# Layout of split fp32 operands in the feed-forward blocks of a decoder trunk: high and low parts mixed by elements or by fours

## The chip, the cores and the metric

One core of a Trainium2 chip runs the whole program. The metric is the device time of one launch in microseconds; the median of several runs is given, and beside it the time of the one execution that the profiler recorded.

## The reference

The program computes two layers of a decoder trunk for 256 tokens of width 1024 in fp32. Each layer is: a half-step feed-forward block, a token mixer with memory cross-attention, a second half-step feed-forward block.

```python
def swiglu(x, w_in, w_out):
    gate, up = jnp.split(x @ w_in, 2, axis=-1)
    return (jax.nn.silu(gate) * up) @ w_out
...
for i in range(DEPTH):                                   # DEPTH = 2
    x = x + 0.5 * swiglu(rms_norm(x, ffn1_norm_g[i]), ffn1_w_in[i], ffn1_w_out[i])
    ...                                                  # mixer: mLSTM (layer 0), sliding window (layer 1)
    x = x + 0.5 * swiglu(rms_norm(x, ffn2_norm_g[i]), ffn2_w_in[i], ffn2_w_out[i])
```

`w_in` is 1024 x 5632 and `w_out` 2816 x 1024, so there are four feed-forward blocks of the same shape. They are called blocks 1 to 4 here; the first mixer (A) lies between blocks 1 and 2, the second (B) between blocks 3 and 4.

## The kernel before, in words

**Split products.** An fp32 product is computed as three matmuls of the type fp32r. Each operand is split into a high part (a copy rounded to fp32r) and a low part (the operand less its high part). `mm3` (lines 224 to 228) issues high x high (line 225), stationary high x moving low (226) and stationary low x moving high (227) into one PSUM bank. Each of the three matmuls loads its own 128 x 128 stationary operand and streams 256 moving columns; the profile lists the loads as PEld.

**Weights.** `wtile` (215) takes a raw tile `wr` of 128 x 4 x 256 values (512 KB) by DMA on SP's queue into a ring of 5 and calls `split` (206): ScalarE copies it to `wh` (211), VectorE subtracts to `wl` (212). `wh` and `wl` are separate tiles in two rings of 8. `wcols` (221) picks the tile of an input projection.

**Activations.** They are kept transposed, features on partitions, tokens along the free axis. A `Norm` object holds the normalised input of the next stage: `put` receives one of four pieces of 2 x 256 values, calls `split_gain` (239: ScalarE scales and rounds, line 132 through `act`; VectorE makes the low part, 241) into the tiles `xh` and `xl`, in two rings of 4, and sums squares (`square`, `fold`). `chain` later computes the reciprocal norm with four small matmuls, an operation on GpSimd and four broadcast matmuls (line 231). The norm's factor is applied after the products.

**A feed-forward block.** `ffn_in` (471) makes the first half: 11 groups of 256 hidden columns, for each gate and up, two weight tiles each, in all 44 weight tiles and 1056 matmuls with a weight tile as the stationary operand and `x.xh`, `x.xl` moving. After each group `hidden` (473) multiplies with the norm's factor (476), applies SiLU, multiplies gate and up (479) and splits the result (`split_plain`, 244, lines 245 and 246) into tiles `u` of 2 x 256 values. `ffn` (509) then makes the second half: for each of four output pieces six weight tiles (`KG`), 528 matmuls in all, moving the split hidden tiles. Lines 544 and 546 add the result to the residual; `nxt.put` hands it to the next norm.

**Order.** TensorE and SP run in the order in which the program is traced; a small planner (`Weave`) puts chains such as a norm's into the stream of matmuls at estimated times. The order on ScalarE and VectorE follows the tiles' dependencies, which the framework turns into semaphore waits: a tile of a ring is written again once all readers of its old contents are done.

**Where things lie.** Within a tile the values that one matmul reads are side by side: 256 moving values of 4 bytes, or 128 stationary ones. The mixers use the same helpers (`Group`, line 310 onwards; `out_proj`), in part with the activations as the stationary operand.

Of the kernel before, what the change touches and what calls it, by code (L numbers as in the profile page):

```python
# [11 lines left out]
F32R = mybir.dt.float32r  # L12
# [7 lines left out]
P = 128  # L20
T = 256
D = 1024
FF = 2816
# [32 lines left out]


WARM = 18


class Weave:
# [37 lines left out]
def tile_trunk(ctx: ExitStack, tc: tile.TileContext, a, out):  # L99
# [99 lines left out]
    def g(i):  # L199
        return gcol[:, i:i + 1]  # L200
# [2 lines left out]
    pieces = [1]  # L203
    last = [None]

    def split(src, shape):
        hi = mk(whp, shape, F32R, "wh")
        lo = mk(wlp, shape, F32R, "wl")
        n = shape[1] // pieces[0]
        for i in range(pieces[0]):  # L210
            last[0] = nc.scalar.copy(hi[:, i * n:(i + 1) * n], src[:, i * n:(i + 1) * n])  # L211
            tt(out=lo[:, i * n:(i + 1) * n], in0=src[:, i * n:(i + 1) * n],  # L212
               in1=hi[:, i * n:(i + 1) * n].bitcast(F32), op=ALU.subtract)
        return hi, lo

    def wtile(src, nk, ncol=256):
        raw = mk(wrp, [P, nk, ncol], F32, "wr")
        nc.sync.dma_start(raw, src)
        return split(raw, [P, nk, ncol])

    def wcols(w, c0, kh):
        return wtile(w.rearrange("(k p) f -> p k f", p=P)[:, kh * 4:(kh + 1) * 4, c0:c0 + 256], 4)

    def mm3(ps, wh, wl, xh, xl, start, stop):
        nc.tensor.matmul(ps, wh, xh, start=start, stop=False, skip_group_check=True)  # L225
# [13 lines left out]
    def split_gain(src, gc, hi, lo):  # L239
        act(hi, src, AF.Copy, scale=gc)  # L240
        nc.vector.scalar_tensor_tensor(out=lo, in0=src, scalar=gc, in1=hi.bitcast(F32),
                                       op0=ALU.mult, op1=ALU.subtract)

    def split_plain(src, hi, lo):
        nc.scalar.copy(hi, src)
        tt(out=lo, in0=src, in1=hi.bitcast(F32), op=ALU.subtract)
# [6 lines left out]
    def bcast_rows(ps, cols):  # L253
        for h in range(2):
            mmf(ps[:, h * P:(h + 1) * P], cols[:, h:h + 1].to_broadcast([P, P]), ident, P)

    def pair(x):
        return x.unsqueeze(1).to_broadcast([P, 2, T])


    class Norm:


        def __init__(self, gi, rows=True, half=True):
            self.gi, self.rows, self.half, self.rc = gi, rows, half, None
            self.done = False
            self.xT, self.xh, self.xl = [], [], []

        def put(self, xn):
            c2 = len(self.xT)  # L270
            hi, lo = mk(xhp, [P, 2, T], F32R, "xh"), mk(xlp, [P, 2, T], F32R, "xl")
            for m in range(2):
                split_gain(xn[:, m], g(self.gi + 2 * c2 + m), hi[:, m], lo[:, m])
            self.xh.append(hi)
            self.xl.append(lo)
            self.xT.append(xn)
            self.square(xn, c2 == 0)
            if c2 == 3:
                self.fold()
# [118 lines left out]
    x0 = Norm(G_F1)  # L398
# [69 lines left out]

    KG = [(0, 4), (4, 4), (8, 4), (12, 4), (16, 4), (20, 2)]

    def ffn_in(x, w_in, hh, hl, mid=None):

        def hidden(ps):
            t = tmp()
            for m in range(2):
                tt(out=t[:, m], in0=ps[m][:, :T], in1=x.rb, op=ALU.mult)  # L476
            act(t, t, AF.Silu)
            for m in range(2):
                tt(out=t[:, m], in0=t[:, m], in1=ps[m][:, T:], op=ALU.mult)  # L479
            hi, lo = unit(F32R), unit(F32R)  # L480
            split_plain(t, hi, lo)
            hh.append(hi)
            hl.append(lo)

        waiting = []
        for gi in range(11):
            ps = [mo(), mo()]
            for kh in range(2):
                for part in range(2):
                    wh, wl = wcols(w_in, part * FF + gi * 256, kh)  # L490
                    for m in range(2):
                        for k in range(4):
                            kc = kh * 4 + k
                            mm3(ps[m][:, part * T:(part + 1) * T],
                                wh[:, k, m * P:(m + 1) * P], wl[:, k, m * P:(m + 1) * P],
                                x.xh[kc // 2][:, kc % 2], x.xl[kc // 2][:, kc % 2],
                                start=kc == 0 and part == 0, stop=kc == 7)
# [11 lines left out]
    def ffn(x, w_in, w_out, nxt=None, mid=None):  # L509

        pieces[0] = 1
        hh, hl = [], []
        yield from ffn_in(x, w_in, hh, hl, mid)
        w = w_out.rearrange("(k p) f -> p k f", p=P)

        def products(ps, m, kg, wt, start):
            ms = slice(m * P, (m + 1) * P)
            for k in range(kg[1]):
                kc = kg[0] + k
                mm3(ps, wt[0][:, k, ms], wt[1][:, k, ms], hh[kc // 2][:, kc % 2], hl[kc // 2][:, kc % 2],  # L520
                    start=kc == 0 and start, stop=kc == 21)

        for c2 in range(4):
# [23 lines left out]
            if nxt is None:  # L547
                nc.scalar.dma_start(out[:, 2 * c2:2 * c2 + 2], xn)
            else:
                nxt.put(xn)  # L550
        wv.spawn(nxt.chain(), LAT['norm'])


# [95 lines left out]
    def mixer_a(x, nxt):  # L649
# [30 lines left out]
        gh, gl = mk(whp, [P, 8, P], F32R, "wh"), mk(wlp, [P, 8, P], F32R, "wl")  # L680
# [306 lines left out]
    with tc.manual_schedule(engines={mybir.EngineType.PE, mybir.EngineType.SP}):  # L987
        wv.run(program())
# [38 lines left out]
```

## Time and profile before

| | us |
|---|---|
| median of 3 runs | 1013.55 |
| lowest and highest | 1012.36, 1013.79 |
| the profiled execution | 1012.23 |
| its span in the trace | 1010.4 |

| engine | busy us | share of the span |
|---|---|---|
| TensorE matmuls (PE) | 998.5 | 99% |
| TensorE weight loads (PEld) | 980.2 | 97% |
| VectorE (DVE) | 655.5 | 65% |
| ScalarE (ACT) | 519.5 | 51% |
| GpSimd (POOL) | 35.7 | 4% |

Matmuls are pipelined: one that lasts 276 ns in the records does not keep the next from starting about 113 ns after it. So a busy share near 100% says that matmuls follow each other without a pause, not how dense they are; the distance between two starts says that. A row of the timeline has start, duration, engine, line, operation, output <- inputs (moving, stationary), shapes and count. A row of groups has count, busy time, mean duration in ns, and the idle time of the engine ahead of the group with what ended it.

### The profile page before, as it was taken

Reading aid. Unit: us, or ns where it says so; the run is one execution under the profiler, and the core shown is the slowest. Engines: PE = TensorE matmul, PEld = TensorE weight load, DVE = VectorE, ACT = ScalarE, POOL = GpSimd, SP = SyncE. Lnnn points to the kernel's source line nnn. Section 1 sums busy time; section 2 is a strip of 40 time slices with the busy share of each in tenths; the row PEclk is TensorE's granted clock in tenths of the full one; section 3 lists DMA queues with packets and bytes.
Section 4 is the critical chain, followed back from the end, with each engine's and each line's share of the span. In section 5 each row is a group of like instructions: output and inputs, shape, how many; then the busy total and the mean of one; then the engine's idle time right before and its main releaser. Section 6 shows DMA issues by size and latency. Waiting matters only on the chain.

```text
span 1010.4 us, 20624 instructions
## 1 busy us (share of the span) xinstructions
PE 998.5 (99%) x8594; PEld 980.2 (97%) x8594; DVE 655.5 (65%) x1063; ACT 519.5 (51%) x764; POOL 35.7 (4%) x32
## 2 busy tenths in 40 slices
PE   8999999999999999999999999999999999999998
PEld 7999999999999999999999999999987899999998
DVE  6866665577856676665558666656787766666551
ACT  7754445446656554444445544544557754454440
POOL 1200000000001000000000000000121000000000
PEclk9999999999999999999999999999999999999999
DMA  9776656666644566665676666567541347666550
GB/s 308 242 245 200 192 180 185 199 183 179 184 139 133 167 210 195 200 189 170 192 206 205 189 191 201 173 197 198 182 131 66 100 131 220 198 189 185 188 170 21
DMA packets 173204, 182.70 MB, mean 181 GB/s; under 512 B 7124, under 2 KB 168328, under 8 KB 173112
## 3 DMA queue, kind: packets, MB, share of 16 engines
q1 hardware_dynamic: 171872, 179.60, 58.3%
q10 hardware_dynamic: 1016, 1.58, 0.5%
q8 instruction: 67, 1.10, 0.5%
q0 software_dynamic: 224, 0.22, 0.2%
q14 instruction: 25, 0.20, 0.1%
HBM read 180.32 MB, written 1.05 MB: 180 GB/s over the span
## 4 chain that ended last, share of the span: by engine, by line
PE 94%; DVE 3%; ACT 1%; DMA 1%; POOL 0%; issue 0%; SPq 0%; ACTq 0%
PE bank L225 30%; PE bank L226 30%; PE bank L227 30%; PE bank L231 2%; PE bank L236 1%; ACT u L132 1%; DVE wl L212 1%; DMA wr<-in_mem_w_kv_dram 1%; PE bank L961 1%; POOL col L379 0%; DVE col L930 0%; DVE u L383 0%; DVE col L591 0%; PE bank L925 0%; DVE u L946 0%
## 5 line engine op out<-in xcount | busy, mean ns | idle before, releaser
L212 DVE TENSOR_TENSOR wl<-wr,wh 128x1024 fp32r<-128x1024 f32 (+1 forms) x347 | 414.7, 1196 | 279.8 <-ACT wh L211 279.0
L211 ACT CAST wh<-wr 128x1024 fp32r<-128x1024 f32 (+1 forms) x347 | 356.8, 1031 | 393.1 <-PE bank L226 368.9
L225 PE MATMUL bank<-xh,wh 128*128 128x256 f32 x1544 | 429.1, 278 | 0.0
L226 PE MATMUL bank<-xl,wh 128*128 128x256 f32 x1544 | 426.8, 276 | 0.0
L227 PE MATMUL bank<-xh,wl 128*128 128x256 f32 x1544 | 426.8, 276 | 0.0
L226 PEld LDWEIGHTS bank<-xl,wh 128*128 128x128 f32 x1544 | 290.3, 188 | 0.1
L225 PEld LDWEIGHTS bank<-xh,wh 128*128 128x128 f32 x1544 | 290.0, 188 | 0.1
L227 PEld LDWEIGHTS bank<-xh,wl 128*128 128x128 f32 x1544 | 289.9, 188 | 0.0
L225 PE MATMUL bank<-u,wh 128*128 128x256 f32 x896 | 249.3, 278 | 0.0
L226 PE MATMUL bank<-u,wh 128*128 128x256 f32 x896 | 247.6, 276 | 0.0
L227 PE MATMUL bank<-u,wl 128*128 128x256 f32 x896 | 247.6, 276 | 0.0
L225 PEld LDWEIGHTS bank<-u,wh 128*128 128x128 f32 x896 | 168.2, 188 | 1.9 <-issue 1.7
L226 PEld LDWEIGHTS bank<-u,wh 128*128 128x128 f32 x896 | 168.4, 188 | 0.1
L227 PEld LDWEIGHTS bank<-u,wl 128*128 128x128 f32 x896 | 168.3, 188 | 0.0
L225 PE MATMUL bank<-wh,xh 128*128 128x256 f32 x208 | 59.7, 287 | 0.0
L226 PE MATMUL bank<-wl,xh 128*128 128x256 f32 x208 | 57.9, 278 | 0.0
L227 PE MATMUL bank<-wh,xl 128*128 128x256 f32 x208 | 57.9, 278 | 0.0
L476 DVE TENSOR_TENSOR t<-bank,rb 128x256 f32<-128x256 f32 x88 | 36.6, 420 | 7.3 <-PE bank L227 7.3
L225 PEld LDWEIGHTS bank<-wh,xh 128*128 128x128 f32 x208 | 39.1, 188 | 0.5 <-issue 0.3
L226 PEld LDWEIGHTS bank<-wl,xh 128*128 128x128 f32 x208 | 39.1, 188 | 0.1
L227 PEld LDWEIGHTS bank<-wh,xl 128*128 128x128 f32 x208 | 39.0, 187 | 0.0
L479 DVE TENSOR_TENSOR t<-t,bank 128x256 f32<-128x256 f32 x88 | 32.7, 412 | 1.8 <-ACT t L132 1.8
(171 smaller groups left out, 657.5 us busy)
## 6 DMA issues: line engine op xcount, KB each, us to landing
wr<-in_ffn_w_in_dram SPq DMA_DIRECT2D x176, 512.0 KB, 3.6
wr<-in_ffn_w_out_dram SPq DMA_DIRECT2D x80, 512.0 KB, 3.5
wr<-in_a_w_in_dram SPq DMA_DIRECT2D x28, 512.0 KB, 3.9
wr<-in_b_w_in_dram SPq DMA_DIRECT2D x14, 512.0 KB, 4.6
wr<-in_a_w_out_dram SPq DMA_DIRECT2D x12, 512.0 KB, 3.3
wr<-in_b_w_out_dram SPq DMA_DIRECT2D x12, 512.0 KB, 3.4
wr<-in_ffn_w_out_dram SPq DMA_DIRECT2D x16, 256.0 KB, 2.8
wr<-in_mem_w_kv_dram SPq DMA_DIRECT2D x7, 512.0 KB, 8.0
```

The costliest lines, as they stand in the source:

```text
L132: ins = nc.scalar.activation(*args, **kw)
L211: last[0] = nc.scalar.copy(hi[:, i * n:(i + 1) * n], src[:, i * n:(i + 1) * n])
L212: tt(out=lo[:, i * n:(i + 1) * n], in0=src[:, i * n:(i + 1) * n], in1=hi[:, i * n:(i + 1) * n].bitcast(F32), op=ALU.subtract)
L225: nc.tensor.matmul(ps, wh, xh, start=start, stop=False, skip_group_check=True)
L226: nc.tensor.matmul(ps, wh, xl, start=False, stop=False, skip_group_check=True)
L227: nc.tensor.matmul(ps, wl, xh, start=False, stop=stop, skip_group_check=True)
L231: nc.tensor.matmul(ps, lhsT, rhs, start=start, stop=stop, skip_group_check=True)
L236: nc.tensor.transpose(ps, src, ident[:k, :k])
L476: tt(out=t[:, m], in0=ps[m][:, :T], in1=x.rb, op=ALU.mult)
L479: tt(out=t[:, m], in0=t[:, m], in1=ps[m][:, T:], op=ALU.mult)
L961: nc.tensor.matmul(o[es[e], cs], vr[:, i, js], pTs[e][:, src], start=i == 0, stop=i == 1, skip_group_check=True)
```

## The change

The parts of one operand are stored in another way, and each of the four blocks gets a way of its own. `SIDE` keeps high and low parts side by side, `ONES` mixes them element by element (high, low, high, low), `FOURS` in runs of four elements. A matmul then reads every second element, or every second run of four.

| block | weights, first half | weights, second half | norm's activations (offset in elements) | hidden activations |
|---|---|---|---|---|
| 1 | ONES | ONES | SIDE (64) | SIDE |
| 2 | ONES | SIDE | SIDE (0) | FOURS |
| 3 | ONES | ONES | SIDE (32) | ONES |
| 4 | SIDE | SIDE | ONES (64) | ONES |

High and low weights share one tile of 2048 elements in one ring of 8. The eight parts (four pieces, high and low) of a norm's activations share one tile of 16 x 256 + 80 elements with one buffer, written from an offset `at`. In mixed blocks `hidden` splits its two halves by one pair of operations each. Some pools are allocated in another order. The mixers keep SIDE. The number, order and shapes of matmuls and DMAs are the same.

```diff
+XPAD = 80
+SIDE, ONES, FOURS = 0, 1, 4
...
-    xhp = pool("xhp", 4)
-    xlp = pool("xlp", 4)
+    vp = pool("vp", 2)
     up = pool("up", 31)
-    vp = pool("vp", 2)
+    sp = pool("sp", 2)
+    xsp = pool("xsp", 1)
     wrp = pool("wrp", 5)
-    whp = pool("whp", 8)
-    wlp = pool("wlp", 8)
+    wp = pool("wp", 8)
     tp = pool("tp", 7)
-    sp = pool("sp", 2)
...
+    lay = [SIDE]
+    def parts(shape):
+        t, n = mk(wp, [P, 2048], F32R, "w"), shape[1] * shape[2]
+        if lay[0] == SIDE:
+            return [t[:, o:o + n].rearrange("p (k f) -> p k f", k=shape[1]) for o in (0, 1024)]
+        v = t[:, :2 * n].rearrange("p (k f e) -> p e k f", k=shape[1], e=2)
+        return [v[:, 0], v[:, 1]]
     def split(src, shape):
-        hi = mk(whp, shape, F32R, "wh")
-        lo = mk(wlp, shape, F32R, "wl")
+        hi, lo = parts(shape)
...
+    def block(wt, k, m):
+        return [w[:, k, m * P:(m + 1) * P] for w in wt]
...
+    def grouped(x, c):
+        return x.rearrange("p (g c) -> p g c", c=c) if c == FOURS else x
+    def mixes(flat, c):
+        if c == ONES:
+            v = flat.rearrange("p (m t e) -> p e m t", m=2, e=2)
+        else:
+            v = flat.rearrange("p (m g e c) -> p e m g c", m=2, e=2, c=c)
+        return v[:, 0], v[:, 1]
...
         def put(self, xn):
             c2 = len(self.xT)
-            hi, lo = mk(xhp, [P, 2, T], F32R, "xh"), mk(xlp, [P, 2, T], F32R, "xl")
+            if c2 == 0:
+                self.tile = mk(xsp, [P, 16 * T + XPAD], F32R, "xs")
+            if self.mixed:
+                c0 = self.at + 4 * c2 * T
+                hi, lo = mixes(self.tile[:, c0:c0 + 4 * T], self.mixed)
+            else:
+                hi, lo = (self.tile[:, c0:c0 + 2 * T].rearrange("p (m t) -> p m t", m=2)
+                          for c0 in (self.at + 2 * c2 * T, self.at + (8 + 2 * c2) * T))
             for m in range(2):
-                split_gain(xn[:, m], g(self.gi + 2 * c2 + m), hi[:, m], lo[:, m])
+                split_gain(grouped(xn[:, m], self.mixed), g(self.gi + 2 * c2 + m), hi[:, m], lo[:, m])
...
             hi, lo = unit(F32R), unit(F32R)
-            split_plain(t, hi, lo)
-            hh.append(hi)
-            hl.append(lo)
+            if mixed:
+                h, l = [], []
+                for m, u in enumerate((hi, lo)):
+                    u = u.rearrange("p a b -> p (a b)")
+                    u = (u.rearrange("p (t e) -> p e t", e=2) if mixed == ONES else
+                         u.rearrange("p (g e c) -> p e g c", e=2, c=mixed))
+                    split_plain(grouped(t[:, m], mixed), u[:, 0], u[:, 1])
+                    h.append(u[:, 0])
+                    l.append(u[:, 1])
+                hh.append(h)
+                hl.append(l)
+            else:
+                split_plain(t, hi, lo)
+                hh.append([hi[:, 0], hi[:, 1]])
+                hl.append([lo[:, 0], lo[:, 1]])
...
-        x1, x2, x3 = Norm(G_MIX, half=False), Norm(G_F2), Norm(G_F1 + 8)
-        x4, x5 = Norm(G_MIX + 8, rows=False), Norm(G_F2 + 8)
-        yield from ffn(x0, a["ffn1_w_in"][0], a["ffn1_w_out"][0], x1, late_constants)
+        x1, x2, x3 = Norm(G_MIX, half=False), Norm(G_F2, at=0), Norm(G_F1 + 8, at=32)
+        x4, x5 = Norm(G_MIX + 8, rows=False), Norm(G_F2 + 8, mixed=ONES)
+        yield from ffn(x0, a["ffn1_w_in"][0], a["ffn1_w_out"][0], x1, late_constants, (ONES, ONES))
         yield from mixer_a(x1, x2)
-        yield from ffn(x2, a["ffn2_w_in"][0], a["ffn2_w_out"][0], x3)
-        yield from ffn(x3, a["ffn1_w_in"][1], a["ffn1_w_out"][1], x4, rope_tables)
+        yield from ffn(x2, a["ffn2_w_in"][0], a["ffn2_w_out"][0], x3, None, (ONES, SIDE), FOURS)
+        yield from ffn(x3, a["ffn1_w_in"][1], a["ffn1_w_out"][1], x4, rope_tables, (ONES, ONES), ONES)
         yield from mixer_b(x4, x5)
-        yield from ffn(x5, a["ffn2_w_in"][1], a["ffn2_w_out"][1])
+        yield from ffn(x5, a["ffn2_w_in"][1], a["ffn2_w_out"][1], None, None, (SIDE, SIDE), ONES)
```

More of the change, by code (lines that the diff above doesn't have):

```diff
@@ L261, in tile_trunk, with __init__ @@
     class Norm:
-        def __init__(self, gi, rows=True, half=True):
-            self.gi, self.rows, self.half, self.rc = gi, rows, half, None
+        def __init__(self, gi, rows=True, half=True, at=64, mixed=SIDE):
+            self.gi, self.rows, self.half, self.rc, self.at, self.mixed = gi, rows, half, None, at, mixed
             self.done = False
@@ L469, in tile_trunk, with ffn_in @@
     KG = [(0, 4), (4, 4), (8, 4), (12, 4), (16, 4), (20, 2)]
-    def ffn_in(x, w_in, hh, hl, mid=None):
+    def ffn_in(x, w_in, hh, hl, mid, mixed):
         def hidden(ps):
@@ L489, in ffn_in @@
                 for part in range(2):
-                    wh, wl = wcols(w_in, part * FF + gi * 256, kh)
+                    wt = wcols(w_in, part * FF + gi * 256, kh)
                     for m in range(2):
@@ L493, in ffn_in @@
                             kc = kh * 4 + k
-                            mm3(ps[m][:, part * T:(part + 1) * T],
-                                wh[:, k, m * P:(m + 1) * P], wl[:, k, m * P:(m + 1) * P],
+                            mm3(ps[m][:, part * T:(part + 1) * T], *block(wt, k, m),
                                 x.xh[kc // 2][:, kc % 2], x.xl[kc // 2][:, kc % 2],
@@ L507, in ffn_in, with ffn @@
                 wv.spawn(mid())
-    def ffn(x, w_in, w_out, nxt=None, mid=None):
+    def ffn(x, w_in, w_out, nxt=None, mid=None, lays=(SIDE, SIDE), mixed=SIDE):
         pieces[0] = 1
         hh, hl = [], []
-        yield from ffn_in(x, w_in, hh, hl, mid)
+        lay[0] = lays[0]
+        yield from ffn_in(x, w_in, hh, hl, mid, mixed)
+        lay[0] = lays[1]
         w = w_out.rearrange("(k p) f -> p k f", p=P)
         def products(ps, m, kg, wt, start):
-            ms = slice(m * P, (m + 1) * P)
             for k in range(kg[1]):
                 kc = kg[0] + k
-                mm3(ps, wt[0][:, k, ms], wt[1][:, k, ms], hh[kc // 2][:, kc % 2], hl[kc // 2][:, kc % 2],
+                mm3(ps, *block(wt, k, m), hh[kc // 2][kc % 2], hl[kc // 2][kc % 2],
                     start=kc == 0 and start, stop=kc == 21)
@@ L679, in mixer_a @@
         nc.sync.dma_start(raw, w.rearrange("(k p) f -> p k f", p=P)[:, :, 3072:3080])
-        gh, gl = mk(whp, [P, 8, P], F32R, "wh"), mk(wlp, [P, 8, P], F32R, "wl")
+        gh, gl = parts([P, 8, P])
         nc.vector.memset(gh.bitcast(F32), 0.0)
```

1 line of the change is left out of this document (added).

## The prediction

> **What bounds the kernel now.** I read the page first: the share of the engines, then the forty slices, then the chain that ended last.
>
> ```profile
> span 1010.4 us, 20624 instructions
> PE 998.5 (99%) x8594; PEld 980.2 (97%) x8594; DVE 655.5 (65%) x1063; ACT 519.5 (51%) x764; POOL 35.7 (4%) x32
> ...
> PEclk9999999999999999999999999999999999999999
> ...
> PE 94%; DVE 3%; ACT 1%; DMA 1%; POOL 0%; issue 0%; SPq 0%; ACTq 0%
> PE bank L225 30%; PE bank L226 30%; PE bank L227 30%; PE bank L231 2%; PE bank L236 1%; ACT u L132 1%; DVE wl L212 1%; DMA wr<-in_mem_w_kv_dram 1%; PE bank L961 1%; POOL col L379 0%; DVE col L930 0%; DVE u L383 0%; DVE col L591 0%; PE bank L925 0%; DVE u L946 0%
> ```
>
> TensorE is the bound, at full granted clock, and nine tenths of the chain are the three matmuls of `mm3` (lines 225 to 227). So I asked next whether TensorE waits for anything, and what its list of waits shows is small:
>
> ```profile
> engine line waited for: us in total, times, longest us
> PE bank L231 <- ACT u L132: 1.5, 1, 1.5
> PE bank L925 <- ACT u L132: 1.4, 1, 1.4
> PE bank L406 <- DVE t L403: 1.3, 1, 1.3
> PE bank L231 <- ACT t L603: 1.1, 1, 1.1
> PE bank L226 <- DVE wl L212: 0.9, 1, 0.9
> ```
>
> Nothing in it belongs to a feed-forward block. The time of these blocks is therefore a number of matmuls times the distance from one start to the next. A busy share hides that distance, so I read it from the timeline of TensorE, in the first feed-forward block, and shortly after a norm's small matmuls at 226 us:
>
> ```profile
> 100.05 0.28 PE L225 MATMUL bank<-xh,wh 128*128 128x256 f32 x1
> ...
> 102.09 0.28 PE L225 MATMUL bank<-xh,wh 128*128 128x256 f32 x1
> ```
>
> ```profile
> 226.02 0.28 PE L225 MATMUL bank<-xh,wh 128*128 128x256 f32 x1
> ...
> 228.02 0.28 PE L227 MATMUL bank<-xh,wl 128*128 128x256 f32 x1
> ```
>
> Between the first two rows lie 18 starts: 2.04 / 18 = 113.3 ns each. Between the second two lie 17: 2.00 / 17 = 117.6 ns. Shapes, types and clock are the same. A stretch stays at one of the two distances until other matmuls interrupt it, and the blocks run almost wholly at 113.3. Other matmuls of 4-byte data come closer:
>
> ```profile
> 270.11 0.60 PE L236 MATMUL bank<-con,u 128*128 128x128 f32 x4
> 270.54 1.03 PE L231 MATMUL bank<-kT,u 128*128 128x256 f32 x4
> ...
> L236 PE MATMUL bank<-con,u 128*128 128x128 f32 x116 | 16.7, 275 | 0.0
> L231 PE MATMUL bank<-kT,u 128*128 128x256 f32 x32 | 8.3, 382 | 1.5 <-ACT u L132 1.5
> ```
>
> Four transposes take 0.60 us from the first start to the last end; less the last one's own 0.275 and over three distances that is 108.3 ns, for 128 moving columns and a weight load of 128 x 128 for every one. The four plain fp32 products of 256 columns give (1.03 - 0.382) / 3 = 216 ns, so plain fp32 takes a column in about twice the time of the fp32r form in `mm3`. A load of 128 x 128 thus fits into 108.3 ns beside a moving stream at half the rate; beside one at full rate the pair takes 113.3 or 117.6. These extra 5.0 or 9.3 ns are what a layout could touch. My reading is that the reads of the two operands get in each other's way, the more often the more one overtakes the other; two stable values for one instruction fit a meeting of two streams that depends on how they are lined up, and fit a fixed cost of changing the weights less well.
>
> **The change part by part.** How many matmuls: one feed-forward block has 11 x 2 x 2 x 2 x 4 x 3 = 1056 in its first half and 22 x 8 x 3 = 528 in its second, 1584 in all and 6336 in four blocks. All keep their number and order. What changes is the step at which each operand is read. Side by side, the 256 moving columns cover 1024 bytes of a partition while the 128 stationary columns of the next load cover 512: one stream overtakes the other. With the weights mixed by elements the load covers 1024 bytes too, and both streams advance at one pace; their starting distance is then kept. That is so in the first halves of blocks 1, 2 and 3 (3 x 1056) and the second half of block 1 (528), where the activations stay side by side: 3696 matmuls. There I cost the full 5.0 ns: 3696 x 5.0 = 18.5 us gained. In the other 2640 (the first half of block 4 and the second halves of blocks 2, 3 and 4, with activations by fours or by elements) the paces differ again, and no row tells which way it goes: between 5.0 ns less each (13.2 us gained) and the other distance that the trace shows, 4.3 ns more each (11.4 us lost). I take no change there, since 113.3 is what nearly all such matmuls show now and is near the middle of the two ends. The new offsets of the activation tile (64, 0 and 32 elements in the first halves of blocks 1, 2 and 3, and 80 elements behind the tile) set the distance that is kept, by some hundred bytes. If one of them keeps the two streams on top of each other, that half gains nothing or goes to the other distance: 1056 matmuls are 5.3 us gained or 4.5 us lost. I take the gain for all three, as two streams in step that have given way once stay apart.
>
> The Trainium skill ("TensorE: Matmul & The Clock Gate", section "Step-by-step: what each phase is for") says that the streamed operand and the weight load have independent read ports, so that loading does not take bandwidth from a running matmul. By it the sum here would be zero, and it is a rival below; the spread of 113.3 and 117.6 for one instruction is not what I would expect from it, though no row settles that.
>
> What the other engines do for the weights and activations:
>
> ```profile
> L212 DVE TENSOR_TENSOR wl<-wr,wh 128x1024 fp32r<-128x1024 f32 x329 | 402.3, 1224 | 265.2 <-ACT wh L211 264.4
> ...
> L246 DVE TENSOR_TENSOR u<-t,u 128x512 fp32r<-128x512 f32 x44 | 30.0, 683 | 0.0
> ...
> L246 DVE TENSOR_TENSOR u<-bank,u 128x256 fp32r<-128x256 f32 x16 | 6.7, 417 | 2.8 <-ACT u L245 2.8
> ```
>
> ```profile
> L211 ACT CAST wh<-wr 128x1024 fp32r<-128x1024 f32 x329 | 345.8, 1053 | 368.5 <-PE bank L226 344.3 <-issue 7.7 <-DMA wr<-in_ffn_w_in_dram 6.5
> ...
> L245 ACT CAST u<-t 128x512 fp32r<-128x512 f32 x44 | 27.0, 613 | 0.2 <-DVE t L479 0.2
> ...
> L245 ACT CAST u<-bank 128x256 fp32r<-128x256 f32 x16 | 6.1, 382 | 7.0 <-PE bank L961 3.9 <-PE bank L231 3.0
> ```
>
> ```profile
> 100.00:150.00 50.00, 50.00 (x443) 50.00 (x443) 32.88 (x45) 24.18 (x28) 0.00 (x0) 1.00 0.62 191
> 150.00:200.00 50.00, 50.00 (x443) 50.00 (x442) 28.23 (x35) 23.84 (x29) 0.00 (x0) 1.00 0.65 188
> ```
>
> (Columns of the last: stretch, then busy time of PE, its loads, VectorE, ScalarE, GpSimd, granted clock, DMA share, GB/s. 443 matmuls touch a stretch of 50 us: 441 at 113.3 ns and two at the edges, in the first half of block 1 as in its second.) A weight tile serves 24 matmuls, 24 x 113.3 ns = 2.72 us. ScalarE needs 1.05 and VectorE 1.22 us for its two parts. Mixed by elements, ScalarE writes and VectorE reads and writes at a step of two elements. No row shows such a step: it costs nothing, or up to twice the time where each element needs a fetch that two shared before; a gain is excluded, because the number of elements is the same. I take nothing: the nearest row is line 212 itself, 1.2 ns an element, and it shows no sign that two elements are handled at once. ScalarE could even bear the double: 24.18 + 18.4 tiles x 1.05 = 43.5 us busy in 50. VectorE could not, and is a rival.
>
> `hidden` splits its tile in two parts in blocks 2, 3 and 4, 33 groups: ScalarE 2 x 382 in place of 613 ns, VectorE 2 x 417 in place of 683, 0.15 us each per 10.9 us group, beside the stream of matmuls. It costs nothing while VectorE has its 17 us free in 50; without that cover, 33 x 0.15 = 5 us.
>
> High and low weights now share one tile and one ring of 8 instead of two rings of 8. Both are still freed by the matmuls of the same tile, the low part by its last. If the interleaved parts count as overlapping, line 225 waits for VectorE's low part instead of ScalarE's high part, 1.2 us later; ScalarE's idle time in front of line 211 (344.3 of 368.5 us put down to TensorE freeing tiles) shows that the splits run up to the ring's end ahead, some seven tiles or 19 us, so nothing waits. The DMAs of the weights and SP's order stay as they are.
>
> All eight activation parts now share one tile with a single buffer. The first write of the next norm, on ScalarE's queue, waits for the last reader of the old one; behind it the splits of weights would queue, and TensorE would wait for those. But the last reader is the end of a block's first half (in a mixer, the last projection ahead of `out_proj`), and the next norm's first write comes after at least 132 matmuls of the second, 15 us later. It costs nothing. DMAs move no more bytes.
>
> **The sum** against the profiled execution: its 1012.23 us (1.83 more than its span) less 18.5 is 993.7. The median of the runs shown is 1013.55, 1.32 above it, so the forecast is 995.0 us.
>
> **The rivals.**
>
> *Full gain.* Any mix breaks the meeting of the streams and all 6336 come to 108.3: 31.7 us, 981.9 us beside the median. For it: two stable distances show that lining up matters. Against: five pairings of layouts and three offsets would all have to come out well. I count it with the forecast as the far end of one mechanism.
>
> *No change.* The 5.0 ns is a cost of each change of weights at full rate, whatever the addresses. Then nothing moves: 1013.5 us. For it: 113.3 holds for hundreds of matmuls over many tiles. Against: 117.6.
>
> *More meetings (slower).* Parts mixed by elements spread over twice the bytes, so each operand needs twice the fetches, and two streams that fetch more meet more. The price is the other distance in the trace: 6336 x 4.3 = 27.2 us, 1040.8 us. It decides as soon as more of the 6336 go up than down.
>
> *VectorE becomes the bound (slower).* At double time it needs 32.88 + 18.4 x 1.22 = 55.4 us for 50 us of matmuls in the first halves of blocks 1, 2 and 3 (119.7 us each): 3 x 12.9 = 39 us; in the second halves of 1 and 3, 28.23 + 22.5 = 50.7, another 2 us: 1055 us. It starts at 1.76 times today's 1.22 us; below that nothing shows.
>
> *A moving stream at step two runs at half rate (slower).* The nearest row is the plain fp32 product with 216 ns. Activations by elements meet it in the second half of block 3 and all of block 4, 528 + 1584 = 2112 matmuls: 2112 x 102.7 = 217 us, 1230 us. Two elements of four in every 16 bytes are still used, which speaks against it. The Trainium skill ("SBUF — State Buffer", "Specifications (TRN2)") says lines of 16 bytes need at least two hits each for full bandwidth; by elements has exactly two and by fours has four, so by it neither half rate nor anything else would be lost. No row here shows it.
>
> **How the numbers follow.** Forecast with its far end: 0.60, own range 982 to 1010. No change: 0.10. More meetings: 0.18. VectorE: 0.06. Half rate: 0.06. So faster by over 0.2% is 0.60, within it 0.10, slower 0.30; 0.2%, some 2 us, is about what a measurement of this kernel can tell from no change. The range goes from the full gain, 982, to more meetings everywhere, 1041, and leaves out the last two cases, 0.12.
>
> **What would show it.** All of block 1 and the first halves of blocks 2 and 3 should have starts near 108 ns apart. With *no change* all halves stay at 113.3; with *more meetings* those with mixed operands show 117 or more; with VectorE as the bound, TensorE waits for `wl` in its list of waits and line 212 takes over 2.1 us; with half rate, block 4 alone has starts some 216 ns apart. The forecast is wrong if the weights' layout alone, in block 1, does not shorten the distance.

## The result, and the profile after

| | before | changed |
|---|---|---|
| median, us | 1013.63 (4 runs) | 1285.58 (4 runs) |
| lowest and highest, us | 1012.36, 1013.79 | 1283.40, 1285.95 |
| span of the profiled execution, us | 1010.4 | 1283.4 |

The changed kernel is slower: ratio 1.2682, 95% interval 1.2660 to 1.2704. From the page of its profile, the span, the engines, the granted clock by slices and the chain that ended last:

```profile
span 1283.4 us, 20654 instructions
...
PE 1271.2 (99%) x8594; PEld 1211.8 (94%) x8594; DVE 663.3 (52%) x1096; ACT 539.1 (42%) x797; POOL 32.8 (3%) x32
...
PEclk9999999999999999999999999999999999999999
...
PE 92%; DVE 4%; ACT 1%; POOL 1%; DMA 1%; issue 0%; SPq 0%; ACTq 0%; POOLq 0%
```

As many matmuls as before, TensorE busy to 99%, and 272.7 of the 273.0 us by which the span is longer are TensorE's busy time. It hardly waits for another engine: its list of waits is as short as before, no entry is over 1.4 us, and the four longest, shown here, belong to other lines than the three matmuls of `mm3` (now 237 to 239).

```profile
PE bank L969 <- ACT u L131: 1.4, 1, 1.4
PE bank L243 <- ACT u L131: 1.3, 1, 1.3
PE bank L437 <- DVE t L434: 1.3, 1, 1.3
PE bank L243 <- ACT t L647: 1.1, 1, 1.1
```

So the matmuls lie further apart. The table by stretches shows where; the columns are the stretch, then busy time and (count) of PE, its loads, VectorE, ScalarE, GpSimd, then granted clock, DMA share, GB/s. The stretches lie in the first half of block 1, the second half of block 2, the first and the second half of block 3, and the first half of block 4:

```profile
100.00:150.00 50.00, 50.00 (x419) 50.00 (x418) 30.12 (x40) 23.66 (x26) 0.00 (x0) 1.00 0.57 177
500.00:550.00 50.00, 50.00 (x427) 50.00 (x426) 28.60 (x33) 23.99 (x29) 0.00 (x0) 1.00 0.62 190
600.00:650.00 50.00, 50.00 (x419) 50.00 (x418) 31.34 (x46) 24.91 (x32) 0.00 (x0) 1.00 0.58 183
700.00:750.00 50.00, 50.00 (x221) 47.18 (x219) 15.97 (x19) 12.90 (x16) 0.00 (x0) 1.00 0.32 97
1000.00:1050.00 50.00, 50.00 (x219) 45.30 (x218) 16.75 (x24) 12.51 (x16) 0.00 (x0) 1.00 0.30 95
```

The busy column says 50.00 in every row; the count tells the rows apart. It includes about two matmuls that began before the stretch, so 444 or 443 in 50 us stands for 113.3 ns between starts, 427 for 117.8, 419 for 50 / 416.6 = 120.0, and 219 for 50 / 217.1 = 230. The granted clock is 1.00 throughout. The timeline of the last stretch agrees: ten starts in 2.30 us.

```profile
1000.18 0.42 PE L238 MATMUL bank<-xs,w 128*128 128x256 f32 x1
...
1002.48 0.42 PE L239 MATMUL bank<-xs,w 128*128 128x256 f32 x1
```

By halves of the blocks, with the distances of the two traces, the extra time comes out as follows:

| where | weights, stream | matmuls | ns before | ns after | us more |
|---|---|---|---|---|---|
| first halves of 1, 2, 3; second of 1 | ONES, SIDE | 3696 | 113.3 | 120.0 | 24.6 |
| second half of 2 | SIDE, FOURS | 528 | 113.3 | 117.8 | 2.3 |
| second half of 3 | ONES, ONES | 528 | 113.3 | 228.9 | 61.0 |
| all of 4 | SIDE, ONES | 1584 | 113.3 | 230.0 | 184.8 |

The sum is 272.7 us, and the spans differ by 273.0. The table says where the time went, not yet which operand's layout costs it; and the 2.3 us of the second row may not be the layout's at all, as the section on the offsets shows.

### The profile page after: what moved, and what is told of

It is laid out like the page before. It is cut to its first block, busy times and chain, and to the rows that moved or that the text cites. A ratio compares the mean times of both kernels' runs of the same rounds, so it can differ in the third digit from the quotient of the medians.

```text
span 1283.4 us, 20654 instructions
## 1 busy us (share of the span) xinstructions
PE 1271.2 (99%) x8594; PEld 1211.8 (94%) x8594; DVE 663.3 (52%) x1096; ACT 539.1 (42%) x797; POOL 32.8 (3%) x32
## 4 chain that ended last, share of the span: by engine, by line
PE 92%; DVE 4%; ACT 1%; POOL 1%; DMA 1%; issue 0%; SPq 0%; ACTq 0%; POOLq 0%
PE bank L237 30%; PE bank L239 30%; PE bank L238 30%; PE bank L243 2%; DVE w L220 1%; POOL col L410 1%; ACT u L131 1%; DMA wr<-in_mem_w_kv_dram 1%; PE bank L248 1%; DVE col L405 0%; DVE u L990 0%; DVE col L974 0%; DVE u L414 0%; PE bank L1005 0%; DVE col L408 0%
## 5 line engine op out<-in xcount | busy, mean ns | idle before, releaser
L220 DVE TENSOR_TENSOR w<-wr,w 128x1024 fp32r<-128x1024 f32 (+1 forms) x347 | 415.0, 1197 | 488.6 <-ACT w L219 488.4
L219 ACT CAST w<-wr 128x1024 fp32r<-128x1024 f32 (+1 forms) x347 | 371.8, 1073 | 596.2 <-PE bank L239 572.0
L237 PE MATMUL bank<-xs,w 128*128 128x256 f32 x1544 | 488.6, 316 | 0.0
L239 PE MATMUL bank<-xs,w 128*128 128x256 f32 x1544 | 486.1, 315 | 0.0
L238 PE MATMUL bank<-xs,w 128*128 128x256 f32 x1544 | 484.7, 314 | 0.0
L238 PEld LDWEIGHTS bank<-xs,w 128*128 128x128 f32 x1544 | 305.8, 198 | 7.7
L239 PEld LDWEIGHTS bank<-xs,w 128*128 128x128 f32 x1544 | 305.2, 198 | 7.6
L237 PEld LDWEIGHTS bank<-xs,w 128*128 128x128 f32 x1544 | 304.6, 197 | 7.7
L237 PE MATMUL bank<-u,w 128*128 128x256 f32 x896 | 304.1, 339 | 0.0
L239 PE MATMUL bank<-u,w 128*128 128x256 f32 x896 | 302.6, 338 | 0.0
L238 PE MATMUL bank<-u,w 128*128 128x256 f32 x896 | 302.0, 337 | 0.0
L237 PEld LDWEIGHTS bank<-u,w 128*128 128x128 f32 x896 | 178.5, 199 | 8.0 <-issue 1.7
L238 PEld LDWEIGHTS bank<-u,w 128*128 128x128 f32 x896 | 178.2, 199 | 6.0
L239 PEld LDWEIGHTS bank<-u,w 128*128 128x128 f32 x896 | 177.9, 199 | 6.1
L237 PE MATMUL bank<-w,xs 128*128 128x256 f32 x208 | 59.8, 288 | 0.0
L239 PE MATMUL bank<-w,xs 128*128 128x256 f32 x208 | 58.0, 279 | 0.0
L238 PE MATMUL bank<-w,xs 128*128 128x256 f32 x208 | 58.0, 279 | 0.0
L257 ACT CAST u<-t 128x256 fp32r<-128x256 f32 (+1 forms) x77 | 34.1, 446 | 31.9 <-DVE t L510 31.9
L237 PEld LDWEIGHTS bank<-w,xs 128*128 128x128 f32 x208 | 39.1, 188 | 0.5 <-issue 0.3
L238 PEld LDWEIGHTS bank<-w,xs 128*128 128x128 f32 x208 | 39.1, 188 | 0.2
L239 PEld LDWEIGHTS bank<-w,xs 128*128 128x128 f32 x208 | 39.0, 188 | 0.0
```

The costliest lines, as they stand in the source:

```text
L238: nc.tensor.matmul(ps, wh, xl, start=False, stop=False, skip_group_check=True)
L239: nc.tensor.matmul(ps, wl, xh, start=False, stop=stop, skip_group_check=True)
```

## The experiments

Two questions were open: what it is in a layout that makes a stream (the moving operand) or a load (the stationary one) slow, and what the 113.3 ns of before are made of. Below, run lengths are in elements; 0 is side by side and 1 by elements. The four numbers of a list are blocks 1 to 4. The diffs are shortened to what they set. A time without a number of runs is that of a single run; the readings rest on the distances in its trace. The letters of the theories are those of the expectations.

### One part of the change alone

```diff
 # weights_only: weights as changed, activations SIDE
-x4, x5 = Norm(G_MIX + 8, rows=False), Norm(G_F2 + 8, mixed=ONES)
+x4, x5 = Norm(G_MIX + 8, rows=False), Norm(G_F2 + 8, mixed=SIDE)
-yield from ffn(x2, ..., None, (ONES, SIDE), FOURS)        # blocks 3 and 4 likewise: ONES -> SIDE
+yield from ffn(x2, ..., None, (ONES, SIDE), SIDE)
 # acts_only: activations as changed, weights SIDE
-yield from ffn(x2, ..., None, (ONES, SIDE), FOURS)        # blocks 1 and 3 likewise: (ONES, ONES) -> (SIDE, SIDE)
+yield from ffn(x2, ..., None, (SIDE, SIDE), FOURS)
```

> The layout of the weights as changed (by elements in both halves of blocks 1 and 3 and in the first half of block 2), all activations side by side. Theory F (fetches: a stationary operand read at step two costs more fetches, and these collide with the stream): starts 120.0 ns apart, as in the changed kernel's first halves, in all 4224 matmuls with mixed weights, whatever the activations' offset; 4224 x 6.7 ns = 28 us more than before, some 1042 us. Theory P (the prediction's: two streams at one pace keep their distance): offsets 64, 0 and 32 should differ from each other, at least one half below 113.3 ns, and the time be under 1013 us.

> The layout of the activations as changed (block 4's norm and the hidden tiles of blocks 3 and 4 by elements, block 2's hidden tiles by fours), all weights side by side. If the moving operand's step alone makes the half rate: 230 ns in 528 + 1584 matmuls, about 117.7 ns in block 2's second half, 113.3 elsewhere; 2112 x 116.7 + 528 x 4.4 ns = 249 us more, some 1262 us. If it needs mixed weights beside it in block 3: that half falls back to 113.3 ns and the time is near 1200 us.

`weights_only` took 1039.76 us (4 runs; ratio 1.0261, interval 1.0244 to 1.0279), `acts_only` 1266.77. Stretches of `weights_only` in the first halves of blocks 1, 2 and 3, with the norm's activations at offsets 64, 0 and 32:

```profile
100.00:150.00 50.00, 50.00 (x419) 50.00 (x419) 30.52 (x40) 23.41 (x25) 0.00 (x0) 1.00 0.56 179
400.00:450.00 50.00, 50.00 (x419) 50.00 (x419) 29.61 (x39) 24.83 (x27) 0.00 (x0) 1.00 0.58 182
600.00:650.00 50.00, 50.00 (x419) 50.00 (x418) 30.57 (x39) 23.95 (x26) 0.00 (x0) 1.00 0.60 188
```

419 in each: 120.0 ns at all three offsets. Theory P, the prediction's, falls: two streams at one pace gain nothing, and their starting distance does not matter. Theory F has distance and time right (4224 x 6.7 = 28 us, measured 27.5); whether it is a collision with the stream, as F says, is tested further down. In `acts_only` the second half of block 3 and the first half of block 4 have 219, about 230 ns as in the changed kernel; a mixed stream needs no mixed weights to be slow. One row was not expected: the first half of block 3, side by side on both sides but at offset 32, has 427, 117.8 ns:

```profile
560.00:610.00 50.00, 50.00 (x427) 50.00 (x426) 31.33 (x46) 24.20 (x32) 0.00 (x0) 1.00 0.59 183
680.00:730.00 50.00, 50.00 (x219) 45.30 (x218) 15.95 (x19) 12.27 (x16) 0.00 (x0) 1.00 0.30 94
1000.00:1050.00 50.00, 50.00 (x219) 45.30 (x218) 16.00 (x22) 11.99 (x15) 0.00 (x0) 1.00 0.31 98
```

### What a stream needs: run lengths and starts

```diff
 # stream_runs: all weights SIDE
+x0..x5: mixed (2, 2, 4, 1) at offsets (64, 65, 65, 65); hidden mixed (2, 4, 8, 16)
```

> Weights side by side everywhere. Activations mixed in runs of other lengths: hidden tiles of blocks 1 to 4 in runs of 2, 4, 8 and 16; norm's activations of block 1 in runs of 2 from an even offset (64), of block 2 in runs of 2 from an odd offset (65), of block 3 in runs of 4 from an odd offset (65), of block 4 by elements from offset 65. Theory A (one fetch brings a pair of neighbouring values, 8 bytes): runs of 2 from the even offset at 113 to 118 ns, from the odd offset 230 ns as each value then has its partner's place in a stranger's run; runs of 4 from an odd offset 3 fetches for 4 values, about 170 ns; runs of 4, 8, 16 at even offsets 113 to 118 ns. Theory L (lines of 16 bytes, two hits each needed): by elements and in runs of 2 alike two of four values of a line are used, so runs of 2 at 230 ns at either offset. Theory C (any innermost step but one is slow, places do not matter): runs of 2 and 4 at 113 to 118 ns at either offset.

It took 1574.69 us. First halves of blocks 1, 2 and 3 (runs of 2 from 64, runs of 2 from 65, runs of 4 from 65), with the second halves of blocks 1, 2 and 3 (runs of 2, 4 and 8) between:

```profile
150.00:200.00 50.00, 50.00 (x220) 45.28 (x219) 17.25 (x27) 12.74 (x17) 0.00 (x0) 1.00 0.30 95
300.00:350.00 50.00, 50.00 (x219) 45.28 (x219) 15.75 (x19) 12.27 (x16) 0.00 (x0) 1.00 0.30 95
600.00:650.00 50.00, 50.00 (x220) 45.36 (x219) 17.28 (x26) 12.83 (x17) 0.00 (x0) 1.00 0.30 95
785.00:835.00 50.00, 50.00 (x427) 50.00 (x427) 28.84 (x34) 23.11 (x29) 0.00 (x0) 1.00 0.62 192
950.00:1000.00 50.00, 50.00 (x218) 44.99 (x217) 16.83 (x26) 12.84 (x17) 0.00 (x0) 1.00 0.30 95
1090.00:1140.00 50.00, 50.00 (x427) 50.00 (x426) 29.78 (x35) 22.88 (x29) 0.00 (x0) 1.00 0.62 191
```

Runs of 2 go at half rate from either offset (230.0 and 228.9 ns), so a pair is not the unit (theory A falls). Runs of 4 go at full rate where each begins at a multiple of 16 bytes (117.8 ns) and at half rate where it begins one element later (231 ns), so places matter and theory C falls too. Theory L (what counts is how many values of a line of 16 bytes are used) fits here. Block 4, not shown, has 228.9 ns by elements from offset 65 and 120.4 in runs of 16.

### What a stream needs: steps

```diff
 # stream_steps: all tiles SIDE; the moving operand x of every matmul
+x -> every 2nd (4th, 8th) of its 256 values, the list repeated 2 (4, 8) times
 # long_steps: first halves; the moving operand for contraction part kc
+x.tile[:, c0:c0 + 256 * s][every s-th value], s = 3, 4, 8, 2; c0 = 64 + 16 * ((4096 - 256 * s) * kc // 8 // 16)
```

> All tiles side by side; only the pattern in which a matmul reads its moving operand is changed, so sums are made of the wrong tokens: in block 1 every second value of the 256 and that twice over, in block 2 every fourth value four times, in block 3 every eighth value eight times, in the first half of block 4 the first 128 values twice (step one). Theory A and theory C: 230 ns in blocks 1, 2 and 3 alike, since every column costs one fetch of its own at any step from two up; 113 ns in block 4; 3 x 1584 x 116.7 = 555 us more, some 1568 us. Theory L: step four and eight touch one value of a line, so blocks 2 and 3 come out near 450 ns or more, over 2200 us in all.

> The stream at a step without repeating addresses: first halves of blocks 1 to 4 read 256 values at steps 3, 4, 8 and 2 out of the whole activation tile (the values are others than the reference takes); second halves side by side. Theory V (a stream takes whole aligned groups of four at full rate and anything else one value at a time, about 0.85 to 0.91 ns): 217 to 234 ns at every step; 1013 + 4224 x 117 ns = 1507 us. Theory G (the stream is bound by groups of 16 bytes, 1.8 ns each, as loads are, and the repeated addresses of the last test hid it): 230 ns at step two, near 345 ns at step three, over 430 ns at steps four and eight.

`stream_steps` took 1553.58 us. Steps of 2, 4 and 8 in blocks 1, 2 and 3:

```profile
150.00:200.00 50.00, 50.00 (x220) 45.27 (x219) 16.50 (x24) 12.04 (x14) 0.00 (x0) 1.00 0.30 95
600.00:650.00 50.00, 50.00 (x217) 44.77 (x216) 15.70 (x22) 11.66 (x14) 0.00 (x0) 1.00 0.30 95
1050.00:1100.00 50.00, 50.00 (x231) 47.38 (x230) 17.48 (x24) 12.05 (x14) 0.00 (x0) 1.00 0.32 102
```

230, 233 and 218 ns: one used value in a line takes about as long as two, and not twice as long, so theory L falls in its turn. The control, 128 values side by side read twice, stayed at 113.3. Since the repeated addresses could have hidden a price, `long_steps` (1514.07 us) reads 256 different places: 234 ns at step 3, 233 at step 4, 218 at step 8, 230 at step 2. These are the rows, blocks 1 to 4:

```profile
150.00:200.00 50.00, 50.00 (x215) 44.55 (x214) 16.20 (x22) 11.45 (x15) 0.00 (x0) 1.00 0.31 95
600.00:650.00 50.00, 50.00 (x216) 44.79 (x215) 15.86 (x20) 11.63 (x14) 0.00 (x0) 1.00 0.30 95
900.00:950.00 50.00, 50.00 (x231) 47.37 (x231) 18.17 (x24) 13.61 (x16) 0.00 (x0) 1.00 0.32 95
1350.00:1400.00 50.00, 50.00 (x220) 45.28 (x219) 15.68 (x20) 11.52 (x13) 0.00 (x0) 1.00 0.31 95
```

Theory G, which priced each group of 16 bytes and gave 345 ns at step 3 and over 430 at steps 4 and 8, falls. What is left is theory V: a stream takes whole, aligned groups of four fp32 values at full rate, and anything else value by value, 218 to 234 ns for 256 values. That it goes value by value is read off these nearly equal times; no trace shows a single fetch.

### What a load needs

```diff
 # load_steps: activations SIDE; step 2a: four k-blocks woven a at a time in the weight tile
+v = t[:, :2 * n].rearrange("p (k f a e) -> p e a k f", a=a, k=shape[1] // a, e=2)
+steps, first halves (2, 4, 8, 1), second halves (4, 8, 2, 1)
 # short_stream: the same with steps (1, 2, 4, 8) in both halves, and in each matmul
-moving 256 columns
+moving 32 columns
 # shorter_stream: weights (SIDE, step 2, SIDE, step 2), moving (128, 128, 192, 192) columns
```

> Activations side by side; the weights of four 128-column blocks woven together so that a load reads at step 2, 4 or 8 (step 2, 4, 8, 1 in the first halves of blocks 1 to 4 and 4, 8, 2, 1 in the second halves). Theory Q (an operand is read in whole aligned groups of four values, 16 bytes, or else value by value): any step from two up makes 128 fetches per load where side by side makes 32, so all mixed halves come out at 120.0 ns and the time at 1013 + 4752 x 6.7 ns = 1045 us. Theory N (what counts is the number of 16-byte lines touched: 32 side by side, 64 at step two, 128 at steps four and eight): step two 120.0 ns, steps four and eight clearly more, some 133 ns; 1013 + 1584 x 6.7 + 3168 x 20 ns = 1087 us.

> Each matmul of the feed-forward blocks streams 32 columns in place of 256 (each column block of the sum gets one part of the contraction only, so seven eighths of the products are left out); weights side by side in block 1 and at steps 2, 4 and 8 in blocks 2, 3 and 4. The load of weights is then the longest thing and its own price stands alone. If a load at a step is longer by itself: starts 7 ns or more further apart in blocks 2 to 4 than in block 1. If it only collides with a full stream: the same distance in all four blocks, near 108 ns or less. If at a step it fetches at half rate, as the stream does: about twice the distance.

> Each matmul streams 128 columns (blocks 1 and 2) or 192 (blocks 3 and 4) of 256, so part of the products is left out; weights side by side in blocks 1 and 3, at step two in blocks 2 and 4. Theory O (a load at step two is bound by its own 64 lines of 16 bytes at some 1.85 ns each, the rate that steps four and eight showed: 233 / 128): 118 to 120 ns in blocks 2 and 4 whatever the stream, and 107 to 110 ns in blocks 1 and 3. Theory K (it collides with the stream): at 128 columns both layouts near 107 ns, at 192 in between. If a shorter fp32r stream is slower per column, or the clock is cut, all four tell nothing on this and the document says so.

`load_steps` took 1424.94 us. First halves of blocks 1, 2 and 3, steps 2, 4 and 8:

```profile
100.00:150.00 50.00, 50.00 (x419) 50.00 (x419) 30.75 (x40) 25.45 (x26) 0.00 (x0) 1.00 0.57 175
500.00:550.00 50.00, 50.00 (x216) 50.00 (x216) 22.52 (x21) 20.26 (x13) 0.00 (x0) 1.00 0.31 95
900.00:950.00 50.00, 50.00 (x209) 50.00 (x208) 22.98 (x20) 19.75 (x13) 0.00 (x0) 1.00 0.30 91
```

120.0, 233.3 and 241.7 ns. The second halves, not shown, repeat it: 235.5, 241.0 and 120.0 ns at steps 4, 8 and 2. Theory Q falls; theory N has the right order with a far too small price. Step 2 touches 64 groups of 16 bytes for 128 values and is only 6.7 ns worse than side by side; steps 4 and 8 touch 128 and double. Divided by groups, 120.0 / 64 = 1.88, 233.3 / 128 = 1.82 and 241.7 / 128 = 1.89 ns: one price per group fits all three, while side by side (32 groups) something else is longer. VectorE and ScalarE are no part of it, though a mixed weight tile takes VectorE 1811 ns on average here: the longest entry of TensorE's list of waits is again 1.4 us.

`short_stream` took 1719.21 us. In most of it TensorE's granted clock was 0.50:

```profile
100.00:150.00 50.00, 50.00 (x236) 50.00 (x236) 15.48 (x22) 12.10 (x14) 0.00 (x0) 0.50 0.36 116
600.00:650.00 50.00, 50.00 (x236) 50.00 (x236) 13.65 (x20) 12.54 (x14) 0.00 (x0) 0.50 0.21 64
950.00:1000.00 50.00, 50.00 (x216) 50.00 (x215) 18.31 (x23) 16.48 (x11) 0.00 (x0) 0.50 0.24 74
```

213.3 ns side by side and at step 2, 233.3 at step 4, and in block 4, not shown, 238.1 at step 8. But blocks 1, 2 and 4 begin at a granted clock of 1.00, before it falls some 3 to 5 us later. These are the first microseconds of blocks 1 and 2, side by side and at step 2; the first two rows give the granted clock (third figure from the end), and the shape 128x32 says that 32 columns move:

```profile
35.30:37.80 2.50, 2.50 (x25) 2.50 (x24) 1.70 (x4) 1.77 (x3) 1.85 (x1) 1.00 0.82 220
508.40:512.80 4.40, 4.40 (x41) 4.40 (x39) 4.40 (x9) 4.40 (x9) 0.00 (x0) 1.00 0.02 8
```

```profile
35.27 0.26 PE L247 MATMUL bank<-xs,w 128*128 128x32 f32 x1
...
37.73 0.26 PE L248 MATMUL bank<-xs,w 128*128 128x32 f32 x1
```

```profile
508.40 0.27 PE L247 MATMUL bank<-xs,w 128*128 128x32 f32 x1
...
512.75 0.28 PE L248 MATMUL bank<-xs,w 128*128 128x32 f32 x1
```

From the first row to the second lie 22 distances in the first pair, 2.46 / 22 = 111.8 ns side by side, and 37 in the second, 4.35 / 37 = 117.6 ns at step 2. With seven eighths of the stream gone the loads still lie this far apart, so this is their own time, and step 2 adds 5.8 ns to it without a full stream to collide with. In block 4 starts at step 8 lie 238 ns apart at the clock of 1.00 and 238.1 at 0.50. So the plain load nearly doubles with half the clock (111.8 to 213.3 ns), and the price per group does not follow it. Why the clock fell is not shown; with 128 columns, below, it stayed.

`shorter_stream` (1022.54 us) kept its clock. Blocks 1 to 4:

```profile
100.00:150.00 50.00, 50.00 (x451) 50.00 (x449) 33.42 (x45) 24.43 (x29) 0.00 (x0) 1.00 0.66 195
400.00:450.00 50.00, 50.00 (x427) 50.00 (x426) 30.51 (x39) 24.67 (x26) 0.00 (x0) 1.00 0.62 184
600.00:650.00 50.00, 50.00 (x450) 50.00 (x450) 33.38 (x45) 24.77 (x29) 0.00 (x0) 1.00 0.63 194
900.00:950.00 50.00, 50.00 (x425) 50.00 (x424) 31.26 (x41) 24.64 (x27) 0.00 (x0) 1.00 0.57 176
```

Side by side 111.7 ns with either stream, at step 2 117.8 with 128 columns and 118.3 with 192. Half the stream away takes only 1.7 to 2.2 ns off. Theory O holds in the main, though its 107 to 110 ns side by side came out as 111.7: most of the step's price, and most of the 113.3 ns, is the load's own and no meeting with the stream. Theory K, and the collision of theory F, fall with it.

### The offsets, and the rest of the change

```diff
 # everything SIDE
+offsets_a: norm's activations at (16, 48, 24, 40)
+offsets_b: (65, 66, 8, 56)
+rest:      (64, 64, 64, 64)
```

> Everything side by side; the norm's activations start at 16, 48, 24 and 40 elements in blocks 1 to 4. So far side by side gave 113.33 ns at offsets 64 and 0 and 117.78 at 32. Theory P2 (the starts' distance, repeating every 256 bytes, decides how often the load's and the stream's fetches meet): other values than these two may come out, down to 108 ns. Theory S (only two states exist): 113.3 or 117.8 ns at every offset; 0 to 4 halves at 117.8, 1013 to 1032 us.

> As before with offsets 65, 66, 8 and 56 elements in blocks 1 to 4. Theory Q with whole groups of four that must also be aligned for each instruction: at 65 and 66 each matmul begins inside a group, and if alignment of the start is needed for the full rate, these halves come out near 230 ns (1013 + 2112 x 117 ns = 1260 us); if a stream only pays for the two broken groups at its ends, they stay at 113 to 120 ns. At 8 and 56: 113.3 or 117.8 by theory S, anything from 108 up by theory P2.

> Everything side by side and every offset 64: of the change only the shared tiles, the single buffer for activations and the other order of the pools are left. If these cost nothing, as the prediction had it: 1012 to 1014 us, all halves at 113.3 ns. If the single buffer or the shared tiles add waits, over 1016 us with entries in TensorE's list of waits that the kernel before does not have.

`offsets_a` took 1038.22 us and `offsets_b` 1043.49. The worst first half, at offset 65, and the one at 66:

```profile
100.00:150.00 50.00, 50.00 (x413) 50.00 (x412) 30.17 (x40) 22.50 (x26) 0.00 (x0) 1.00 0.58 183
400.00:450.00 50.00, 50.00 (x419) 50.00 (x418) 29.61 (x39) 22.49 (x26) 0.00 (x0) 1.00 0.59 181
```

By the means of the starts the eight offsets give: 16, 120.0; 48, 118.7; 24, 116.7; 40, 120.0; 65, 121.7; 66, 120.0; 8, 118.3; 56, 118.7 ns. Offsets 64 and 0 gave 113.3 and 32 gave 117.8. So there are more than two values (theory S falls), the offset does matter when both operands are side by side, up to 8.4 ns, and 113.3 ns, which the kernel before has already, is the best of eleven offsets, most of them seen in a single run. Whether it is the distance of the two starts or the stream's own start that matters is not separated. A start inside a group (65, 66) does not cost the half rate: only groups that are broken throughout do.

The value 117.8, however, does not tell one layout from another. Everything side by side with offset 64 gave it in both halves of block 4 of `load_steps` (first row). And the second half of block 2, where only hidden tiles move, has it in `offsets_a` (second row) and 113.3 in `rest` (third row), though the two kernels differ in the norm's offsets alone:

```profile
1250.00:1300.00 50.00, 50.00 (x427) 50.00 (x427) 31.50 (x42) 23.64 (x28) 0.00 (x0) 1.00 0.62 188
490.00:540.00 50.00, 50.00 (x427) 50.00 (x426) 28.73 (x34) 22.96 (x29) 0.00 (x0) 1.00 0.64 191
475.00:525.00 50.00, 50.00 (x444) 50.00 (x443) 30.05 (x36) 23.82 (x29) 0.00 (x0) 1.00 0.67 197
```

What chooses between the two values stays open. So the 117.8 ns at offset 32, and of the activations by fours, may be this second value and no price of the layout.

`rest` leaves of the change only the shared tiles, the single buffer and the order of the pools. Its profiled execution took 1011.51 us, every half at 113.3 ns, no new wait. Its median over 12 runs is 1018.65 (1011.51 to 1026.58) and the ratio 1.0044 (1.0018 to 1.0069), above the 1012 to 1014 expected, if by less than 1%. The kernel before took 1018.30 us in one of the 17 runs beside it. One first half at 117.8 instead of 113.3 ns would make 4.7 us and one second half 2.4, and the rows above show either value for one layout. That would explain the spread, but no trace of a longer run was taken, so it is argued and not shown.

No version among these is faster than the kernel before.

## Why the prediction was wrong, by its own steps

**What bounds the kernel** was right: matmuls times the distance of their starts, nothing waiting. **The reading of the 5.0 ns** over the transposes' 108.3 as two streams meeting was wrong in the main: with half the stream gone 3.4 of the 5.0 ns are still there (111.7), and with seven eighths gone 3.5 (111.8). They belong to the load, which is nearer to the rival *no change*. Why the loads of the transposes fit into 108.3 ns stays open. The part that does depend on how the starts lie exists (the offsets), but the kernel before already had the best value found.

**Equal pace gains 5.0 ns in 3696 matmuls**: this step failed first. It gave -18.5 us and measured +24.6, because a load at step two touches 64 groups of 16 bytes in place of 32 and its own time becomes the longer one; with 32, 128 and 192 moving columns it costs 5.8, 6.1 and 6.6 ns more, with 256 6.7. The three offsets made no difference to it. That the two operands keep one pace, the reason given for the gain, plays no part.

**No change in the other 2640**: this is the step that cost the forecast. It gave 0 and measured 2.3 us (528 by fours) and 245.8 us (2112 by elements), because a stream by elements runs at half rate, 228.9 to 230.0 ns. The bounds I put around it, 108.3 to 117.6, came from rows that all read their stream side by side, so neither could stand for a stream at a step. The row that could was the plain fp32 product at 216 ns; I used it for a rival, at 217 us, with a chance of 0.06 and left it outside the range. The rival's 1230 us lack 28.8 us because such a stream takes 229 to 230 ns and not 216, and the 26.9 us of the other rows; its sign in block 4 alone forgot the second half of block 3, which its own count has. What counted against the rival was that two of four values in 16 bytes are still used. The Trainium skill ("SBUF — State Buffer", "Specifications (TRN2)") asks for two hits in a line of 16 bytes for full bandwidth. The loads here agree nearly: 120.0 ns at two hits, 233.3 at one. The streams do not: two hits give 230.0 and one hit 233.3. For a stream the measurement decides: of the patterns run, only whole lines with all four hits kept the rate.

**More meetings** as a rival had the right sign for the 3696 (4.3 ns given, 6.7 measured), but not the mechanism. The Trainium skill ("TensorE: Matmul & The Clock Gate", "Step-by-step: what each phase is for") has independent ports for stream and load; the 1.7 ns between a half and a full stream agree in the main, and the prediction gave the rule too little weight. The up to 8.4 ns that an offset costs are not explained by it.

**The other engines** were right. VectorE's weight tile takes 1225 ns where it took 1224, though in mixed halves it reads one operand and writes at step two; ScalarE's 1097 where it took 1053. These means mix the layouts; in the first half of block 1 alone, where all weights are mixed, they are 1226 and 1137 ns, before 1055 on ScalarE:

```profile
L220 DVE TENSOR_TENSOR w<-wr,w 128x1024 fp32r<-128x1024 f32 x329 | 402.6, 1225 | 453.0 <-ACT w L219 452.8
```

```profile
L219 ACT CAST w<-wr 128x1024 fp32r<-128x1024 f32 x329 | 360.4, 1097 | 550.4 <-PE bank L239 526.9 <-issue 12.4 <-ACT t L131 3.3
```

**Shared tiles and the single buffer** cost no wait, as said. Beyond that, the 0.44% of `rest` was not foreseen.

## What to carry to other kernels

Keep the moving fp32r operand of a matmul in whole, aligned groups of 16 bytes: by elements or in pairs it streamed at half rate here (229 to 230 ns in place of 113), and a chain of matmuls took twice as long with no engine waiting. A stationary operand at step two costs some 6% of the distance between starts (120.0 ns in place of 113.3), at step four it doubles it (233.3). When a change alters an operand's access pattern, take the bound from a row that reads in the new pattern; if there is none, the slow end belongs into the range, however unlikely it looks.

## What the runs showed of the hardware that was not expected

A stream in whole aligned groups of four fp32 values runs at 113 to 122 ns for 256 columns, beside a load that takes 111.7 by itself; one in runs of two, in runs of four that straddle the groups, or at steps 2, 3, 4 and 8 at 218 to 234 ns. The widest step was the least slow (218 ns at step 8). A load of 128 columns takes 111.7 ns side by side, and about 1.85 ns for each group of 16 bytes that it touches where that is longer (an estimate from steps 2, 4 and 8); at a granted clock of 0.50 it takes 213.3 ns at steps one and two alike, and at steps 4 and 8 what it takes at full clock. One layout can run for hundreds of matmuls at 113.3 or at 117.8 ns. VectorE's subtraction at step two took as long as side by side (1226 ns and 1224 ns).
